# A two-layer hybrid backbone: a lagged start, a later place for layer 1's modulation, and S5 in two streams

## The chip, the cores and the metric

The kernel runs on one core of a Trainium2 chip. PE (TensorE) does the matmuls, DVE (VectorE) and ACT (ScalarE) the elementwise work, POOL (GpSimd) little, and SP (SyncE) issues most DMAs. Times are device microseconds of one execution; the metric is the median over several.

## The reference, cut to what matters

512 tokens (256 of context, 256 latent) of width 1024 pass through two layers, all in fp32. Each layer reads six modulation vectors, computed from a conditioning vector for the latent tokens and another for the context:

```
m = silu(c) @ w_mod[l] + b_mod[l]                    # 6 x 1024, w_mod[l] is 1024 x 6144
p = (rms(x) * norm_mix[l] * (1 + m[1]) + m[0]) @ w_in[l]   # split among three mixers and three gates
y = (s5(p), retention(p), gla(p))                    # scans forward and backward, latent after context
x = x + m[2] * (sum_b sigmoid(gate_b) * (y_b @ w_b)) @ w_out[l]
h = rms(x) * norm_ffn[l] * (1 + m[4]) + m[3]
x = x + m[5] * ((silu(h @ w1) * (h @ w2)) @ w_ffn_out[l])
```

In layer 1 only the latent tokens are needed from the mixers on. A final RMSNorm ends it. "Vector lm" below is modulation vector m of layer l: vector 05 is m[5] of layer 0.

## The kernel before

**Products.** A large fp32 product is made from three reduced-precision ones: operand and weight are split into hi and lo, and hi·hi, hi·lo and lo·hi are accumulated in one bank. A weight tile of 128 x 1024 is loaded into one of three `raw` buffers, ACT writes its hi half, DVE subtracts for its lo half (four pairs), and PE uses both. The activations lie in `rb`, hi and lo.

**What sets the order.** Work is written in program order with priorities, and a scheduler that keeps a modelled time per engine settles each engine's order when the program is built. Loads are issued far ahead (`W_AHEAD`). SP's queue is in order, so a load that waits for its buffer holds back all behind it. `issue_after(x)` keeps the instructions inside it behind instruction x on the same engine.

**The start.** `layer(0)` takes four chunks c of 256 columns. `mod_chunk` loads two 1 MB pieces of `w_mod` (vectors 1 and 0), makes their product with silu(c) on PE, evicts the row by ACT and transposes it. `norm_chunk` transposes the normalised tokens, applies scale and shift on DVE in a buffer `h32`, copies the hi half by ACT and subtracts the lo half. `pack_weights` and `pack_mms` then load and multiply chunk c of the first packed input projection into four banks. `pack_out` evicts them and permutes S5's inputs for a trip through DRAM (`perm`, by DVE from the bank). `load_params2` and `s5_tables` (tables of the S5 scan) follow.

**Modulation vectors on the side.** Vectors 02 to 05 and all of layer 1, besides the S5 tables' rotation and preparation (`rot`, `prep0`, `prep1`), are generators in a list, `side`. `tick`, called in the loops over weights, advances the first of them by one step, `need(name)` drains up to a name. One step of `mod_vec` loads 128 rows of `w_mod` (0.5 MB) into a ring of two tiles `wm`. For vectors 04, 05 and 12 to 15 (`ON_VECTOR`) DVE then accumulates it (one or two operations), and PE sums over partitions at the end (`unit`); for the others PE multiplies it with silu(c) directly. The order was 02, 03, 04, 05, 12, 11, 10, 13, prep1, 14, 15.

**Mixers.** `weave` advances the generators of S5 (`s5_core`, two halves hf of eight groups, one after the other), retention and GLA in turn, one step each. In layer 1 the gates' matmuls lie between them on PE. A half of `s5_core` multiplies inputs by tables, rotates, scans twice, rotates back, and its readout on PE needs both states.

**Layer 1's FFN.** `norm_t` transposes the scaled tokens of one block of 128 (t = 2, 3), applies scale and shift by ACT (half of the columns) and DVE, copies hi by ACT and subtracts lo. `ffn_in_tok` multiplies blocks t in the order (1, 0), i.e. 3 then 2. `ffn_out` runs two passes over the weights in layer 0, one for each half of the tokens, and each ends in `residual` on DVE.

## Time and profile before

| | |
|---|---|
| median of 3 runs | 1385.05 us (1379.94 to 1386.57) |
| profiled execution | 1389.15 us |
| its span | 1387.1 us |
| mean granted clock of PE | 0.986 |
| PE busy | 1332.2 us, 96% |
| DVE busy | 909.6 us, 66% |
| ACT busy | 579.1 us, 42% |
| moved by DMA | 255.63 MB, 184 GB/s |

A timeline row gives the start, the length, the engine, line, operation, result <- operands and count, and in brackets how long the engine was idle before it and what released it. PE's rows overlap, because matmuls are pipelined; the distance of starts tells the pace. PEclk is the granted clock as a share of full speed.

### The profile page before, as it was taken

What the parts mean: (1) busy time and instruction counts of PE and PEld (TensorE: products, weight loads), DVE (VectorE), ACT (ScalarE), POOL (GpSimd) and SP (SyncE); (2) the same over time, 40 slices, a digit from 0 to 9 for tenths busy, and PEclk for the clock granted to TensorE, in tenths of its full rate; (3) what the DMA queues carried; (4) which work ended last, traced back from release to release, by engine and by line L of the source; (5) the groups of instructions that cost most, each with busy time, mean ns of one, the idle gap of its engine ahead of it and who ended that gap; (6) DMA issues with size and microseconds to landing.
All of it is one profiled execution on the core that took longest, in us unless ns stands there. A gap on an engine that the chain in (4) does not pass through costs nothing.

```text
span 1387.1 us, 20296 instructions
## 1 busy us (share of the span) xinstructions
PE 1332.2 (96%) x7723; PEld 1082.7 (78%) x7723; DVE 909.6 (66%) x1395; ACT 579.1 (42%) x920; POOL 73.7 (5%) x115
## 2 busy tenths in 40 slices
PE   4899999999999999999999999999999989899997
PEld 3788888777767778788777777898987867788886
DVE  4579682849879665535455687764696688655555
ACT  3367352333432233222222345544456544544453
POOL 3310000002000020000000000000000010000000
PEclk9999999999999999999999999999999989999999
DMA  9743455677877565633333787654655646465653
GB/s 308 205 123 106 153 167 165 228 220 236 280 245 216 200 184 170 215 92 106 119 115 116 250 310 245 197 158 122 181 160 189 199 145 213 149 194 187 213 183 106
DMA packets 202584, 255.63 MB, mean 184 GB/s; under 512 B 20704, under 2 KB 153100, under 8 KB 201976
## 3 DMA queue, kind: packets, MB, share of 16 engines
q1 hardware_dynamic: 189032, 228.05, 52.6%
q10 hardware_dynamic: 10240, 20.39, 4.1%
q0 software_dynamic: 3216, 5.91, 1.7%
q8 instruction: 61, 1.00, 0.3%
q14 instruction: 35, 0.29, 0.1%
HBM read 231.00 MB, written 23.30 MB: 183 GB/s over the span
## 4 chain that ended last, share of the span: by engine, by line
PE 81%; DMA 8%; DVE 5%; issue 2%; ACT 2%; SPq 1%; POOL 0%; DVEq 0%; ACTq 0%; POOLq 0%
PE b L243 79%; DMA wm<-in_w_mod_dram 4%; PE b L253 2%; DVE arena L231 1%; DVE zone L234 1%; DVE lo L231 1%; DMA arena<-in_w_mod_dram 1%; DMA raw<-in_w_in_dram 1%; ACT arena L228 1%; DMA arena<-udr 1%; ACT hi L228 1%; DMA arena<-sw 1%; DMA arena<-in_ctx_dram 0%; DMA raw<-in_w_ffn_out_dram 0%; DMA rb<-k 0%
## 5 line engine op out<-in xcount | busy, mean ns | idle before, releaser
L243 PE MATMUL b<-hi,rb 128*128 128x512 f32 (+2 forms) x1752 | 535.5, 383 | 5.5 <-DVE arena L593 3.5
L243 PE MATMUL b<-rb,hi 128*128 128x512 f32 (+1 forms) x1568 | 465.3, 378 | 1.4 <-DVE rb L231 1.4
L231 DVE TENSOR_TENSOR lo<-raw,hi 128x1024 fp32r<-128x1024 f32 (+3 forms) x295 | 333.7, 1136 | 201.4 <-ACT hi L228 198.5
L228 ACT ACTIVATE hi<-raw 128x1024 fp32r<-128x1024 f32 (+3 forms) x295 | 289.7, 989 | 419.4 <-PE b L243 275.0
L243 PEld LDWEIGHTS b<-hi,rb 128*128 128x128 f32 x1752 | 328.1, 189 | 67.4 <-issue 8.1
L243 PE MATMUL b<-lo,rb 128*128 128x512 f32 (+2 forms) x876 | 334.2, 382 | 0.9 <-DVE lo L231 0.9
L243 PEld LDWEIGHTS b<-rb,hi 128*128 128x128 f32 x1568 | 284.5, 189 | 64.5 <-issue 11.9
L243 PE MATMUL b<-rb,lo 128*128 128x512 f32 (+1 forms) x784 | 294.2, 376 | 0.0
L243 PEld LDWEIGHTS b<-lo,rb 128*128 128x128 f32 x876 | 166.2, 190 | 28.3 <-issue 1.6
L243 PEld LDWEIGHTS b<-rb,lo 128*128 128x128 f32 x784 | 147.9, 189 | 28.6 <-issue 3.4
L228 ACT ACTIVATE arena<-b 128x512 f32<-128x512 f32 (+7 forms) x168 | 79.1, 481 | 106.1 <-PE b L243 71.8
L243 PE MATMUL b<-arena 128*128 128x96 f32 (+9 forms) x1056 | 120.7, 289 | 0.8 <-ACT arena L228 0.8
L231 DVE TENSOR_TENSOR arena<-arena 128x512 f32<-128x512 f32 (+5 forms) x164 | 102.0, 640 | 17.2 <-ACT arena L228 14.9
L243 PEld LDWEIGHTS b<-arena 128*128 128x128 f32 (+6 forms) x1056 | 89.9, 160 | 24.3 <-issue 8.3
L234 DVE SCALAR_TENSOR_TENSOR arena<-arena,b 128x512 f32<-128x512 f32 (+1 forms) x124 | 72.3, 587 | 47.4 <-PE b L243 44.3
L234 DVE SCALAR_TENSOR_TENSOR zone<-wm,sil,zone 128x1024 f32<-128x1024 f32 x56 | 71.0, 1280 | 26.1 <-DMA wm<-in_w_mod_dram 26.0
L231 DVE TENSOR_TENSOR zone<-zone 128x512 f32<-128x512 f32 (+3 forms) x117 | 67.9, 604 | 28.5 <-DMA wb<-zone 17.4
L228 ACT ACTIVATE rb<-arena 128x256 fp32r<-128x256 f32 (+3 forms) x101 | 46.4, 476 | 61.5 <-PE b L243 33.6
L231 DVE TENSOR_TENSOR rb<-arena,rb 128x256 fp32r<-128x256 f32 (+2 forms) x106 | 53.7, 521 | 16.9 <-ACT rb L228 16.7
L253 PE MATMUL b<-cst,arena 128*128 128x128 f32 (+2 forms) x254 | 40.0, 284 | 19.4 <-DMA arena<-in_norm_mix_dram 8.9
L253 PEld LDWEIGHTS b<-cst,arena 128*128 128x128 f32 (+2 forms) x254 | 30.9, 146 | 27.3 <-issue 16.1
L228 ACT ACTIVATE arena<-arena 128x512 f32<-128x512 f32 (+3 forms) x62 | 36.7, 599 | 34.9 <-DVE arena L231 27.8
(145 smaller groups left out, 686.5 us busy)
## 6 DMA issues: line engine op xcount, KB each, us to landing
wm<-in_w_mod_dram SPq DMA_DIRECT2D x80, 512.0 KB
raw<-in_w_ffn_out_dram SPq DMA_DIRECT2D x66, 512.0 KB
raw<-in_w_in_dram SPq DMA_DIRECT2D x48, 512.0 KB
raw<-in_w_ffn_in_dram SPq DMA_DIRECT2D x44, 512.0 KB
raw<-in_w_ffn_in_dram SPq DMA_DIRECT2D x88, 256.0 KB
raw<-in_w_in_dram SPq DMA_DIRECT2D x48, 384.0 KB
raw<-in_w_out_dram SPq DMA_DIRECT2D x16, 512.0 KB
arena<-in_w_mod_dram SPq DMA_DIRECT2D x7, 1024.0 KB
```

What stands on the lines that cost most here:

```text
L228: self.S.activation(out, in_, f, bias=bias, scale=scale)
L231: self.last = self.V.tensor_tensor(out=out, in0=a, in1=b, op=op).ins
L234: self.last = self.V.scalar_tensor_tensor(out=out, in0=a, scalar=s, in1=b, op0=op0, op1=op1).ins
L243: self.last_mm = self.P.matmul(out, l, r, start=start, stop=stop, **k).ins
L253: self.last_tr = self.P.transpose(out, in_, self.ident[:k, :k]).ins
```

## The change

1. *Start.* The eight loads of `mod_chunk` become sixteen of half the rows. In the loop the packed matmuls lag one chunk: modulation and norm of chunk c, then `pack_mms` of c-1. Chunk c's weights and their splits stay behind the eviction of its modulation row on ACT. `norm_chunk` lets ACT write hi straight from the bank with scale and shift, while DVE makes h32 and lo. `load_params2` and `s5_tables` stand behind the last packed matmul on PE, the tables on ACT behind the last norm.
2. *Modulation.* The order is 02, 03, 04, 05, 11, 10, 12, 13, prep1, 14, 15; those from 12 on are closed until step 2 of layer 0's `ffn_in`, and their instructions stand behind that step's DVE instruction.
3. *Layer 1's packing.* The perm copies read ACT's SBUF copy in place of the bank.
4. *Mixers of layer 1.* Two S5 generators, one for each half, the second three rounds late, and retention first; part of the second half's buffers lie in `zone`.
5. *Layer 1's FFN norm.* hi is written from the bank by ACT; in the first piece of `ffn_in_tok` each block's products with the weights come block by block, the block's lo last.

```diff
@@ act, tick, aside
+        self.closed = ("mod12", "mod13", "prep1", "mod14", "mod15")
+        self.behind = None
...
     def tick(self):
-        if self.side:
-            with self.inside(self.zone):
+        if self.side and not (self.closed and self.side[0][0] in self.closed):
+            with self.inside(self.zone), self.tc.issue_after(self.behind) if self.behind else nullcontext():
@@ mod_chunk
         for m in (1, 0):
             ws[m] = (self.zone if c == 3 and m else self.arena).new(KD, 256)
-            self.q["modc"].dma_start(out=ws[m].ap, in_=i["w_mod"][0][:, D * m + 256 * c:D * m + 256 * c + 256].rearrange(
-                "(k p) c -> p k c", p=128))
+        for kh in range(2):
+            for m in (1, 0):
+                self.q["modc"].dma_start(out=ws[m].ap[:, 4 * kh:4 * kh + 4], in_=i["w_mod"][0][
+                    512 * kh:512 * kh + 512, D * m + 256 * c:D * m + 256 * c + 256].rearrange("(k p) c -> p k c", p=128))
...
         self.act(rows.ap, b[:, :128], AF.Copy)
+        self.row_out = self.last_act
@@ norm_chunk
-            self.tt(hv, b.rearrange("p (t k c) -> p t k c", t=2, k=2), bc(self.mod[:, 0, 1]), ALU.mult)
-            self.tt(hv, hv, bc(self.mod[:, 0, 0]), ALU.add)
-        self.act(self.rb[:, 1:5, 0, ks], h32.ap, AF.Copy)
-        self.tt(self.rb[:, 1:5, 1, ks], h32.ap, self.rb[:, 1:5, 0, ks].bitcast(F32), ALU.subtract)
+            for k in range(2):
+                kk = 2 * c + k
+                src = b[:, 256 * k:256 * k + 256].rearrange("p (t c) -> p t c", t=2)
+                self.act(self.rb[:, rows, 0, kk], src, AF.Identity, scale=sc[:, kk, s:s + 1], bias=sh[:, kk, s:s + 1])
+                self.ts(h32.ap[:, :, k], src, sc[:, kk, s:s + 1], sh[:, kk, s:s + 1], ALU.mult, ALU.add)
+            self.tt(self.rb[:, rows, 1, ks], h32.ap, self.rb[:, rows, 0, ks].bitcast(F32), ALU.subtract)
@@ norm_t
-                if k < 2:
-                    self.act(dst, src, AF.Identity, scale=sc[:, kk, s:s + 1], bias=sh[:, kk, s:s + 1])
-                else:
-                    self.ts(dst, src, sc[:, kk, s:s + 1], sh[:, kk, s:s + 1], ALU.mult, ALU.add)
-            self.act(self.rb[:, 1 + t, 0, ks], h32.ap[:, ks], AF.Copy)
+                self.act(self.rb[:, 1 + t, 0, kk], src, AF.Identity, scale=sc[:, kk, s:s + 1], bias=sh[:, kk, s:s + 1])
+                self.ts(h32.ap[:, kk], src, sc[:, kk, s:s + 1], sh[:, kk, s:s + 1], ALU.mult, ALU.add)
@@ pack_out
-            perm(up.ap[:, c0:], banks[x][:, c0:])
+            perm(up.ap[:, c0:], (o.ap if lean else banks[x])[:, c0:])
@@ ffn_in
+            if f == 2 and l == 0:
+                self.closed, self.behind = (), self.last
             self.tick()
@@ ffn_in_tok, first piece
-                self.tok_mms(banks, ws, (1, 0), range(KD), 0, KD - 1, h)
+                for t in (1, 0):
+                    for k in range(KD):
+                        for x in range(2):
+                            self.mm_(banks[t], h(t, k)[0], ws[k // 2][x][:, k % 2], k == 0 and x == 0, False)
+                    for k in range(KD):
+                        self.mm_(banks[t], h(t, k)[1], ws[k // 2][0][:, k % 2], False, k == KD - 1)
@@ layer
                 for c in range(4):
                     self.mod_chunk(c, brow)
                     self.norm_chunk(c, xs)
-                    self.pack_mms(banks, self.pack_weights(0, 0, c), c)
+                    with self.tc.issue_after(self.row_out):
+                        ws.append(self.pack_weights(0, 0, c))
+                    if c:
+                        self.pack_mms(banks, ws[c - 1], c - 1)
+                self.pack_mms(banks, ws[3], 3)
...
-            self.asides("2345cbadpef")
+            self.asides("2345bacdpef")
...
-        self.weave(("srg", "rsg")[l], g=gla, s=self.s5_core(l, self.s5d[l], u_dr, t0),
-                   r=self.ret(l, rqk, rv, ro, t0))
+        if last:
+            self.weave("rstg", g=gla, s=core(0), t=self.late(3, core(1)), r=ret)
+        else:
+            self.weave("srg", g=gla, s=core(0, 1), r=ret)
```

**ACT at the start, chunks 1 to 3.** `raw` and `hi` are a weight tile and its split half (chunk 0's is the first), `b_249`, `b_343` and `b_437` before are the banks of the modulation rows of chunks 1, 2 and 3. Before:

```order
L228 ACTIVATE hi_313<-raw_310 128x16x48
L228 ACTIVATE hi_313<-raw_310 128x16x16
L228 ACTIVATE arena<-b_249 128x128
L228 ACTIVATE rb<-arena 128x4x256
L228 ACTIVATE hi_407<-raw_404 128x16x48
L228 ACTIVATE hi_407<-raw_404 128x16x16
L228 ACTIVATE hi_501<-raw_498 128x16x48
L228 ACTIVATE hi_501<-raw_498 128x16x16
L228 ACTIVATE arena<-b_343 128x128
```

And now, with the rows of chunks 1, 2 and 3 in `b_231`, `b_331` and `b_431`:

```order
L230 ACTIVATE arena<-b_231 128x128
L230 ACTIVATE hi_301<-raw_298 128x16x48
L230 ACTIVATE hi_301<-raw_298 128x16x16
L230 ACTIVATE rb<-b_278,mod 128x2x128
L230 ACTIVATE rb<-b_288,mod 128x2x128
...
L230 ACTIVATE arena<-b_331 128x128
L230 ACTIVATE hi_401<-raw_398 128x16x48
L230 ACTIVATE hi_401<-raw_398 128x16x16
L230 ACTIVATE rb<-b_378,mod 128x2x128
...
L230 ACTIVATE arena<-b_431 128x128
L230 ACTIVATE hi_501<-raw_498 128x16x48
```

Each row's eviction now stands ahead of its chunk's split; before, chunk 2's stood behind two of them.

**SP at vector 05's last loads.** A merge weight tile is loaded in three pieces (`w_br_...`). Before, the last two steps of vector 05 are `wm_3280` and `wm_3316`, and `wm_3403` is vector 12's first:

```order
L273 DMA raw_3588<-in_w_br_gla_dram 128x3x128
...
L357 DMA wm_3280<-in_w_mod_dram 128x1024
L273 DMA raw_3636<-in_w_br_s_dram 128x2x128
L273 DMA raw_3636<-in_w_br_ret_dram 128x3x128
L273 DMA raw_3636<-in_w_br_gla_dram 128x3x128
L357 DMA wm_3316<-in_w_mod_dram 128x1024
L357 DMA wm_3403<-in_w_mod_dram 128x1024
```

And now, where they are `wm_3304` and `wm_3340`:

```order
L359 DMA wm_3268<-in_w_mod_dram 128x1024
L275 DMA raw_3525<-in_w_br_s_dram 128x2x128
L275 DMA raw_3525<-in_w_br_ret_dram 128x3x128
L275 DMA raw_3525<-in_w_br_gla_dram 128x3x128
...
L359 DMA wm_3304<-in_w_mod_dram 128x1024
L359 DMA wm_3340<-in_w_mod_dram 128x1024
L275 DMA raw_3576<-in_w_br_s_dram 128x2x128
```

Three merge weight tiles fewer stand ahead of vector 05's last load. In PE's order, counted in 512-column matmuls, vector 05's final matmuls stood at 1052, and the tile just ahead of its last load was used from 1134 on; now at 995 and 1062. Vector 11's products stood from 1197 to 1398 and vector 10's from 1446 to 1542; now from 1022 to 1182 and from 1230 to 1398.

**PE at the end of layer 1's mixers.** `rb,hi` and `hi_...` rows with 512 columns are the gates' matmuls, rows that read only `arena` are GLA's, `b_8544<-rb,arena` (now `b_8570`) is S5's readout. Before:

```order
L243 MATMUL b_8417<-arena 128x256 x2
L243 MATMUL b_9141<-hi_9163,rb 128x512 x2
...
L243 MATMUL b_8421<-arena 128x256 x2
L243 MATMUL b_8425<-arena 128x96 x2
L243 MATMUL b_8456<-arena,rb 128x64 x8
L243 MATMUL b_9141<-lo_9200,rb 128x512
...
L243 MATMUL b_8425<-arena 128x96 x6
L243 MATMUL b_8467<-arena,rb 128x64 x8
L243 MATMUL b_8478<-arena 128x128 x2
L243 MATMUL b_9218<-hi_9221,rb 128x512 x2
...
L243 MATMUL b_8516<-arena 128x96
L243 MATMUL b_8544<-rb,arena 32x128 x20
```

And now:

```order
L245 MATMUL b_8486<-arena 128x256 x2
L245 MATMUL b_9244<-hi_9265,rb 128x512
...
L245 MATMUL b_9243<-hi_9265,rb 128x512
L245 MATMUL b_8490<-arena 128x256 x2
L245 MATMUL b_8494<-arena 128x96 x2
L245 MATMUL b_8512<-arena 128x128 x2
L245 MATMUL b_8494<-arena 128x96 x6
L245 MATMUL b_8516<-arena 128x128 x2
L245 MATMUL b_8520<-arena 128x96
...
L245 MATMUL b_8570<-rb,arena 32x128 x7
...
L245 MATMUL b_8570<-rb,arena 32x128 x4
L255 MATMUL b_8600<-cst,arena 128x64 x4
```

Before, gate matmuls stood between the steps of GLA's last chunk (from place 3608 to 3660); now its state stands at 3653 and all later steps in one piece behind place 3660, ahead of S5's readout's end.

## Rows read from the trace of the kernel before

**Rows 1.** The page's first part: busy us, share of the span, instructions.
```profile
PE 1332.2 (96%) x7723; PEld 1082.7 (78%) x7723; DVE 909.6 (66%) x1395; ACT 579.1 (42%) x920; POOL 73.7 (5%) x115
```

**Rows 2.** The windows: stretch, length, busy by engine, PEclk, DMA share, GB/s.
```profile
0.00:35.00 35.00, 15.94 (x214) 12.62 (x215) 15.73 (x45) 11.58 (x26) 13.30 (x29) 1.00 1.00 308
35.00:70.00 35.00, 31.11 (x236) 25.39 (x237) 19.17 (x41) 10.74 (x17) 10.84 (x21) 0.90 0.72 207
...
105.00:140.00 35.00, 33.21 (x215) 30.77 (x214) 32.45 (x59) 25.73 (x41) 2.21 (x4) 1.00 0.38 118
...
385.00:420.00 35.00, 32.00 (x155) 23.93 (x154) 28.27 (x31) 10.85 (x16) 0.00 (x0) 0.95 0.74 234
...
770.00:840.00 70.00, 69.85 (x365) 54.18 (x364) 53.12 (x63) 30.71 (x48) 0.00 (x0) 1.00 0.86 290
...
1120.00:1155.00 35.00, 30.59 (x157) 24.22 (x158) 29.91 (x54) 17.96 (x36) 3.76 (x2) 0.86 0.51 168
```

**Rows 3.** PE's timeline from 8 to 66 us: start, length, work, idle before.
```profile
41.35 1.07 PE L243 MATMUL b<-arena,sil 128*32 128x128 f32 x30
44.90 0.48 PE L253 MATMUL b<-cst,arena 128*128 128x128 f32 x1 [2.47 <-ACT arena L228]
...
47.01 0.65 PE L243 MATMUL b<-wm,one 1*32 1x128 f32 x8
...
51.63 0.33 PE L253 MATMUL b<-cst,arena 128*128 128x128 f32 x1 [0.40 <-ACT arena L228]
...
54.91 0.50 PE L243 MATMUL b<-rb,hi 128*128 128x512 f32 x1 [1.02 <-DVE rb L231]
...
59.55 1.30 PE L243 MATMUL b<-rb,hi 128*128 128x512 f32 x5
...
65.00 0.35 PE L243 MATMUL b<-hi,rb 128*128 128x416 f32 x1
```

**Rows 4.** ACT's timeline from 40 to 53 us.
```profile
43.54 1.15 ACT L228 ACTIVATE hi<-raw 128x768 fp32r<-128x768 f32 x2 [7.21 <-DMA raw<-in_w_in_dram]
44.59 0.26 ACT L228 ACTIVATE arena<-b 128x128 f32<-128x128 f32 x1
```

**Rows 5.** PE's timeline at vector 05 and at vector 10.
```profile
405.33 0.64 PE L243 MATMUL b<-zone,unit 128*32 128x256 f32 x8 [2.23 <-DVE zone L234]
...
517.08 0.64 PE L243 MATMUL b<-wm,sil 128*32 128x256 f32 x8 [1.78 <-DMA wm<-in_w_mod_dram]
```

**Rows 6.** SP's queue at 399 us and DVE's timeline from 399 to 412 us.
```profile
399.24 2.55 SPq L357 DMA_DIRECT2D wm<-in_w_mod_dram  x2
...
403.99 2.48 DVE L234 SCALAR_TENSOR_TENSOR zone<-wm,sil,zone 128x1024 f32<-128x1024 f32 x2 [1.43 <-DMA wm<-in_w_mod_dram]
```

**Rows 7.** PE's timeline between layer 0's two passes of ffn_out.
```profile
845.37 0.50 PE L243 MATMUL b<-hi,rb 128*128 128x512 f32 x1 [1.07 <-DVE arena L231]
```

**Rows 8.** PE's timeline behind the packing of layers 0 and 1.
```profile
109.24 0.44 PE L243 MATMUL b<-hi,rb 128*128 128x384 f32 x1 [1.79 <-DVE arena L593]
...
972.06 0.41 PE L243 MATMUL b<-hi,rb 128*128 128x384 f32 x1 [1.70 <-DVE arena L593]
```

**Rows 9.** PE's timeline at the end of layer 1's mixers.
```profile
1121.86 1.93 PE L243 MATMUL b<-rb,arena 128*32 128x128 f32 x32 [3.00 <-DVE arena L231]
```

**Rows 10.** DVE's timeline in the same place.
```profile
1112.34 2.33 DVE L1122 TENSOR_TENSOR_SCAN arena<-arena 128x512 f32<-128x512 f32 x2
...
1120.36 1.44 DVE L231 TENSOR_TENSOR arena<-arena 64x504 f32<-64x504 f32 x3
```

**Rows 11.** PE's timeline at layer 1's FFN norm.
```profile
1186.54 1.06 PE L253 MATMUL b<-cst,arena 128*128 128x128 f32 x8 [1.79 <-DVE arena L238]
1190.01 1.94 PE L253 MATMUL b<-cst,arena 128*128 128x128 f32 x8 [2.41 <-DVE arena L238]
1191.61 0.78 PE L243 MATMUL b<-hi,rb 128*128 128x512 f32 x1
```

**Rows 12.** DVE's groups by line and shape: count, busy us, mean ns, idle before.
```profile
L231 DVE TENSOR_TENSOR arena<-arena 128x512 f32<-128x512 f32 x118 | 79.3, 685 | 15.2 <-ACT arena L228 14.5
```

More of the change, by code (lines that the diff above doesn't have):

```diff
@@ L227, in act @@
     def act(self, out, in_, f, scale=1.0, bias=0.0):
-        self.S.activation(out, in_, f, bias=bias, scale=scale)
+        self.last_act = self.S.activation(out, in_, f, bias=bias, scale=scale).ins
     def tt(self, out, a, b, op):
@@ L406, in weave, with late @@
                         del gens[c]
+    @staticmethod
+    def late(n, gen):
+        for _ in range(n):
+            yield
+        yield from gen
     def aside(self, name, gen):
@@ L598, in pack_out @@
             self.act(o.ap[:, c0:], banks[x][:, c0:], AF.Copy)
-            perm(up.ap[:, c0:], banks[x][:, c0:])
+            if lean and x == 0:
+                self.act(o.ap[0:64, 0:256], banks[0][0:64, 0:256], AF.Copy)
+            perm(up.ap[:, c0:], (o.ap if lean else banks[x])[:, c0:])
             for s in range(2):
@@ L1077, in s5_core @@
         nn = 64 - n0
-        u8 = self.new(16, 64)
-        for hf in range(2):
+        for hf in hfs:
+            u8 = self.new(8, 64)
             gs = slice(8 * hf, 8 * hf + 8)
@@ L1112, in s5_core @@
             c, s = rot.ap[:, 0], rot.ap[:, 1]
-            rr, ri, t = big.new(8, 64), big.new(8, 64), big.new(8, 64)
+            tmp = self.zone if l and hf else big
+            rr, ri, t = tmp.new(8, 64), tmp.new(8, 64), tmp.new(8, 64)
             self.tt(rr.ap, X[0].ap, c, ALU.mult)
@@ L1128, in s5_core @@
                 self.tt(ri.ap, X[1].ap, b_, ALU.mult)
-                o = self.new(8, 64)
+                o = big.new(8, 64) if x else tmp.new(8, 64)
                 nc.vector.memset(o.ap[0:64, :, 0:1], 0.0)
@@ L1148, in s5_core @@
             self.read_out = self.last_mm
-            if hf == 0:
-                yt = self.yt = self.new(8, 128)
+            if hf == hfs[0] and hfs[0] == 0:
+                self.yt = self.new(8, 128)
+            yt = self.yt
             for gg in range(ng):
```

39 lines of the change are left out of this document (22 added, 17 removed).

## The prediction

> **What bounds the kernel now.** I read the busy times on the page first [rows 1]: PE is busy 1332.2 of 1387.1 us, no other engine above 909.6. The change neither removes nor adds a large matmul, so all it can win are the gaps of PE and the stretches in which PE's granted clock is halved. The table of windows [rows 2] then shows where those are: 35 to 70 us (PE 31.11 of 35, clock 0.90), 105 to 140, 385 to 420 (32.00), and 1120 to 1155 (30.59, clock 0.86). The timeline gives each gap its releaser. From start to start, the 24 512-column matmuls between 59.55 and 65.00 us take 227 ns each [rows 3]. I call that one unit, and count places in PE's order in it.
>
> The profiled execution took 1389.15 us (span 1387.1), 4.10 above the median of 1385.05. The sum is made against 1389.15, and 4.1 is taken off at the end.
>
> **The start (0 to 65 us).** Before, chunk 2's row eviction on ACT stood behind the hi split of chunk 3's weights. That split waited 7.21 us for its DMA, until 43.54, and the eviction followed at 44.59 [rows 4], so PE began chunk 2's transposes at 44.90 after 2.47 idle [rows 3]. Now ACT evicts chunk c's row ahead of that chunk's hi split, and PE has the packed matmuls of chunk c-1 behind chunk c's modulation. What can be won between 41.35 and 65.00 us (23.65 us)? The rows from 44.90 to 51.63 stand in the stretch of halved clock: the norm took 2.11 and modulation 3 took 4.62 [rows 3], half of which is 1.05 and 2.3. At full clock the work between 41.35 and 65.00 is then 1.0 of modulation 2, two norms of 1.05, 2.3 and two chunks of 5.45: 16.3. The rest, 7.3 us, is idle time (2.47, 0.40, 1.02) and half clock. Modulation 3's weights stand ahead of the load that ended 43.54, so they were there by then, and in the new order PE still has chunk 1's or 2's matmuls to do while they land. I take **-7.3**. The ends are -3 (only the two waits of 2.47 and 1.02 go, less a new one of 0.5 on ACT) and -9 (a finish at about 56, modulation 3 at 41.8 with 2.3, 5.45, 1.05 and 5.45 of work from there, 14.3). The norm of a chunk drops the copy of 1024 columns on ACT and two passes on DVE, and evicts straight from the bank. Four evictions of 256 take the copy's place. PE covers both. The DVE work of the S5 tables starts when packing ends. It shifts along as long as it is not itself the bound: DVE is busy 32.45 of 35 us in 105 to 140 [rows 2], which is the first rival.
>
> The w_mod chunks now come in halves, eight more DMAs. In the first 35 us the DMA share is 1.00 at 308 GB/s [rows 2], with transfers of 1 MB and less mixed in one queue, so the row shows no gap that more transfers would add to: zero. The Trainium skill, page "DMA: Bandwidth & Descriptors", section "Anatomy of one DMA", speaks against it: it states a fixed cost near 2.0 us for each DMA beside the bytes, measured on the GpSimd path. Eight of those in series would be 16 us and turn the sum to about 1389; a share of 1.00 says that they overlap.
>
> **The order of the modulations.** Before, vector 12 was built on DVE and vectors 11 and 10 on PE behind it; now 11 and 10 come first, and 12, 13, the S5 preparation, 14 and 15 wait for the third step of layer 0's FFN. Each step has its price:
> - Vector 10's last loads no longer run into the FFN. PE's wait of 1.78 for one of them at 517.08 [rows 5] goes: **-1.9** with its restart.
> - Vector 05's final matmuls move from unit 1052 to 995, 57 earlier. The load that was waited for (issued 399.24, used by DVE from 403.99 after a wait of 1.43, PE idle 2.23 before 405.33 [rows 5, 6]) moves too. It stood behind a merge weight used at unit 1134, 82 units after its own use, and now stands behind one used at 1062, 67 after: 15 units or 3.4 us more time. The waits there are 2.8 in all. I take **-1.5**, between -2.8 and +3 (DVE does not keep up, 28.27 of 35 busy [rows 2]).
> - Vector 11 on PE reads its loads directly, in the stretch where DMA is 0.74 busy. The ring holds two tiles, so a load is issued when the one two places ahead has been used. At four places of the new order that leaves 24 to 26 units, 5.4 to 5.9 us, between that use and the load's own use. Issue to use was 4.75 us in one case [rows 6]. It was more where PE waited at 517.08 [rows 5]. So **+1.5**, from 0 to +4.
> - The closed work lands in the FFN. DVE instructions of 1.24 us each [rows 6] (8 for vector 12) leave the crowded merge and go where nothing waits for them. In ffn_out the loads of 14 and 15 now cross the boundary of the two passes, where DMA is 0.86 busy at 290 GB/s and PE already waited 1.07 before 845.37 [rows 2, 7]. Zero; it costs up to +5 if the cover is gone (second rival).
>
> **Layer 1's packing.** The copies that held a bank until DVE had them now read SBUF, and ACT frees the bank. PE's 1.70 before 972.06 [rows 8] falls to about 0.5: **-1.2**, from -1.7 to 0. Layer 0 keeps its own wait of 1.79 before 109.24, since nothing there changes.
>
> **S5 in two streams.** Before, the second half's DVE steps came last (scans 1112.34, its differences 1120.36 [rows 10]), and PE waited 3.00 for them at 1121.86 [rows 9]. Now that half runs beside the first, three rounds later, so the 3.00 goes. But GLA's last state matmuls move from unit 3608 to 3653, and the gate matmuls that filled PE end at unit 3660. Where 52 units lay between the steps of GLA's last chunk, 7 are left. PE then waits for GLA itself. The nearest row is the wait of 3.00 that S5 had in this place; the far end is a whole S5 half on DVE (10 operations at 0.685 [rows 12], 2.33 of scans, twice 1.44 [rows 10]: 12.1). I take 4 against the 3.00, **+1**, from -3 to +9.
>
> **Layer 1's FFN norm.** The hi half is written from the bank by ACT without an intermediate, and the first products with lo come last. PE waited 1.79 and 2.41 for scaled rows ahead of 1186.54 and 1190.01, and its first FFN matmul came at 1191.61 [rows 11]. The first block's matmuls can now start before the second block's transposes, but in the order only two of them do; the second block's transposes still wait for DVE's scaling. **-2.5**, from 0 to -4.2.
>
> **Sum.** -7.3 -1.9 -1.5 +1.5 -1.2 +1 -2.5 = -11.9. 1389.15 - 11.9 = 1377.25, and less 4.1 it is **1373**.
>
> **Rivals.**
> *The start's gain is lost again behind it.* DVE is 93% busy from 105 to 140 us [rows 2], and PE's wait of 1.79 at 109.24 [rows 8] is DVE's. If the tables are not released earlier by the full 7.3, only the slack of 2.55 of that window stays, and vector 05's matmuls, 13 us earlier, wait 3 longer instead of 1.5 less. That is +4.75 and +4.5: **1382**. For it: the rows of DVE. Against it: DVE was only 19.17 of 35 busy in 35 to 70, so what queues there starts as soon as its input does.
>
> *The boundary in ffn_out.* The loads of vector 15 and its steps of 1.24 on DVE meet the residuals, which DVE also makes; four steps more ahead of them are +5, **1378**. For it: DMA 0.86, DVE 53.12 of 70 [rows 2]. Against: the number of loads in the stage stays.
>
> *The change does not do what it says at the start:* the lagged matmuls wait for their own splits, which now stand behind the rows on ACT; -3 in place of -7.3, and the norm wins nothing: +6.8, **1380**. Against: even chunk 3's split began at 43.54 [rows 4], and its matmuls come last.
>
> *Eight halves cost eight whole transfers.* At 308 GB/s a half takes 1.7 us [rows 2]; eight more of those ahead of chunk 3 put 13.6 on the start: **1387**. A share of 1.00 speaks against it.
>
> *GLA's last chunk stands bare.* With both S5 streams ahead of it in each round on DVE, GLA ends later by a whole half, 12.1, on top of the 4, and the clock falls once more: 0.90 over the window 35 to 70 is a loss of 3.5 us [rows 2]. 12.1 + 4 + 3.5 against 3.00 is +16.6 in place of +1: **1389**, within 0.5%. For it: the new order of PE. Against it: DVE has 29.91 of 35 in that window now, and what it does in total stays.
>
> *Slower: PE waits for vectors 11 and 10 load by load.* With a ring of two, each load is issued only when PE has used the one two places ahead; in the stretch of 0.74 DMA share each of the eight loads of vector 11 then holds PE up by what one did at 517.08, 1.78 [rows 5], 14.2 in all, and the clock falls twice for it, 3.5 each [rows 2]: +21.2 in place of +1.5 is **1393**. It decides against the change from about 13 us of such waits. For it: DVE's wait of 1.43 for one of these loads, which PE now has itself [rows 6]. Against it: only four of the sixteen have under 6 us.
>
> **How the numbers follow.** Chances: forecast 0.57, start lost behind 0.15, boundary 0.08, not what it says 0.07, halves 0.02, GLA bare 0.05, load by load 0.06. The forecast's own range runs from 1361 (start -9, vector 05 -2.8, S5 -3, norm -4.2) to 1380 (start -3, vector 11 +4). To leave no more than 2 in 10 out it goes up to 1385, which takes in the first three rivals with their spread. 0.5% (6.9 us) is what a measurement of this kernel can tell from no change, so faster means under 1378.1 and slower over 1392. Faster: 0.57 without its upper end of 0.05, half of the boundary and the lower spread of the first and third (0.09): 0.65. Slower: load by load and the upper end of GLA bare, 0.08. Same 0.27.
>
> **What would show it.** Right at the start: ACT evicts rows 2 and 3 within a microsecond of PE's modulation, the first matmul of gla_v comes near 57.7 in place of 65.00, and the window 35 to 70 has PE above 33. Wrong: an idle row of several us at the perms near 100, or the window 105 to 140 with more PE idle than 1.8. Modulations: no row of PE waiting for wm near 508, none above 1 us at vector 05, and those of vector 11 below 2 in all. S5: the wait ahead of S5's readout gone, and PE's waits from GLA's last state matmuls to its output add up to 3 to 6. FFN norm: the first FFN matmul 4 to 5 us after the last matmul of the projection. The forecast is wrong altogether if the start moves by less than 3 us.

## The result, and the profile after

The changed kernel takes **1403.82 us** (median of 12 runs, 1393.38 to 1409.58) against 1386.24 of the kernel before in the same comparison: ratio 1.0128, 95% interval 1.0100 to 1.0155. It is slower by 1.3%, where 1373 (1361 to 1385) was forecast. Its profiled execution took 1393.38 (span 1391.3) and was the shortest of the twelve; a second profile, of another execution, took 1403.31 (span 1401.1), which is near the median. The profile of before has a span of 1387.1. Single executions differ: beside the second profile the kernel before took 1396.24 once.

The first part of the page, the first profile, then the second (as [rows 1]):

```profile
PE 1338.3 (96%) x7723; PEld 1083.0 (78%) x7723; DVE 913.1 (66%) x1407; ACT 585.1 (42%) x940; POOL 78.8 (6%) x115
```
```profile
PE 1348.1 (96%) x7723; PEld 1091.7 (78%) x7723; DVE 913.0 (65%) x1407; ACT 585.5 (42%) x940; POOL 78.9 (6%) x115
```

Subtract from the spans: PE was idle 54.9 us before, and 53.0 and 53.0 in the two profiles. **The change did win idle time, 1.9 us. PE's busy time grew instead**, by 6.1 and by 15.9 us, for the same 7723 matmul records. The trace's clock records tell how much of this is clock. Of its busy time PE spent 27.3 us at half clock before, 28.0 in the first profile and 55.6 in the second. If half of such time is lost (an estimate), the clock makes about 14 of the 15.9 us in the second profile, the typical one, and next to nothing of the 6.1 in the first. What those 6.1 are stays open; they are spread over many groups of matmuls. The windows of the first profile (as [rows 2]):

```profile
35.00:70.00 35.00, 31.57 (x222) 26.30 (x215) 24.06 (x61) 13.28 (x24) 8.58 (x17) 0.95 0.69 211
...
385.00:420.00 35.00, 33.01 (x184) 22.23 (x183) 19.47 (x25) 10.68 (x17) 0.00 (x0) 1.00 0.70 212
...
770.00:840.00 70.00, 68.47 (x353) 52.51 (x352) 52.31 (x66) 31.30 (x51) 0.00 (x0) 1.00 0.79 276
...
1120.00:1155.00 35.00, 31.37 (x186) 24.18 (x186) 26.71 (x49) 18.11 (x35) 3.42 (x2) 0.90 0.34 111
```

I compared the traces by place (the count of 512-column units in PE's order, taken at the first large matmul there): how much later than before PE comes through each stretch, in us. A stretch need not hold the same work in both kernels, since small matmuls change places.

| places | what lies there | forecast | first profile | second profile |
|---|---|---|---|---|
| 0–100 | start | −7.3 | −2.9 | −2.6 |
| 100–800 | layer 0's packing and mixers | 0 | +2.1 | +0.9 |
| 800–2900 | vectors: merge, FFN, boundary | −1.9 | −5.0 | −2.4 |
| 2900–3300 | layer 1's packing | −1.2 | +0.1 | 0.0 |
| 3300–3600 | layer 1's mixers | +1 with the next row | +11.8 | **+13.6** |
| 3600–3700 | their end, with GLA's last chunk | | −4.1 | **+3.2** |
| 3700–end | FFN norm, FFN | −2.5 | +2.0 | +1.2 |
| sum | | −11.9 | +4.1 | +14.0 |

The mixers' +7.7 and +16.8 are larger than all the other terms together. Part of the +11.8 and of the −4.1 is work that has changed places: 28 records of small matmuls more stand ahead of place 3600 and 28 fewer behind it. Two things are new. Ahead of place 3600 PE waits 4.3 us in both profiles instead of 0.8, and the clock is halved for 10.2 and 13.7 us where it had been full. Behind place 3600 it is halved for 6.8 and 23.9 us, before for 10.2. So the first profile has its loss ahead of place 3600 alone, and the second on both sides. The window 1000 to 1030 of before, then of the second profile (columns as in [rows 2]):

```profile
1000.00:1030.00 30.00, 29.22 (x195) 25.42 (x194) 26.05 (x48) 15.54 (x24) 0.91 (x1) 1.00 0.55 159
```
```profile
1000.00:1030.00 30.00, 27.48 (x135) 24.06 (x135) 19.19 (x35) 14.21 (x21) 0.00 (x0) 0.77 0.64 176
```

PE's timeline behind place 3600, the first profile, then the second; both rows hold the same 70 records of small matmuls of GLA's last chunk (the built order has 42 matmuls of it, the trace 84 records):

```profile
1111.47 9.03 PE L245 MATMUL b<-arena 48*128 48x256 f32 x70 [0.93 <-DVE arena L236]
```
```profile
1115.41 14.57 PE L245 MATMUL b<-arena 48*128 48x256 f32 x70 [1.58 <-DVE arena L236]
```

### The profile page after: what moved, and what is told of

Read it like the earlier page. It is cut to its first block, busy times and chain, and to the rows that moved or that the text cites. A ratio compares the mean times of both kernels' runs of the same rounds, so it can differ in the third digit from the quotient of the medians.

```text
span 1391.3 us, 20310 instructions
## 1 busy us (share of the span) xinstructions
PE 1338.3 (96%) x7723; PEld 1083.0 (78%) x7723; DVE 913.1 (66%) x1407; ACT 585.1 (42%) x940; POOL 78.8 (6%) x115
## 4 chain that ended last, share of the span: by engine, by line
PE 56%; DVE 5%; DMA 5%; ACT 3%; issue 2%; SPq 0%; POOL 0%; DVEq 0%; POOLq 0%; ACTq 0%
PE b L245 55%; DVE lo L233 2%; DMA raw<-in_w_ffn_out_dram 1%; PE b L255 1%; ACT arena L230 1%; ACT hi L230 1%; DVE arena L233 1%; DMA wm<-in_w_mod_dram 1%; DMA raw<-in_w_in_dram 1%; DVE arena L242 1%; DVE arena L236 1%; DMA raw<-in_w_out_dram 0%; DVE rb L233 0%; DMA udr<-arena 0%; DMA raw<-in_w_br_s_dram 0%
## 5 line engine op out<-in xcount | busy, mean ns | idle before, releaser
L245 PE MATMUL b<-arena 128*128 128x96 f32 (+8 forms) x1064 | 121.7, 289 | 1.3 <-DVE arena L236 0.9
L230 ACT ACTIVATE arena<-b 128x256 f32<-128x256 f32 (+7 forms) x170 | 79.4, 480 | 102.5 <-PE b L245 75.5
L245 PEld LDWEIGHTS b<-arena 128*128 128x128 f32 (+5 forms) x1064 | 91.5, 161 | 25.1 <-issue 8.3
L233 DVE TENSOR_TENSOR arena<-arena 128x512 f32<-128x512 f32 (+4 forms) x162 | 102.3, 645 | 10.4 <-ACT arena L230 8.4
L233 DVE TENSOR_TENSOR zone<-zone 128x512 f32<-128x512 f32 (+4 forms) x122 | 70.5, 605 | 22.7 <-DMA wb<-zone 15.2
L233 DVE TENSOR_TENSOR rb<-arena,rb 128x256 fp32r<-128x256 f32 (+1 forms) x110 | 54.3, 506 | 22.1 <-ACT rb L230 22.0
L230 ACT ACTIVATE rb<-arena 128x256 fp32r<-128x256 f32 (+3 forms) x93 | 40.0, 442 | 52.5 <-PE b L245 38.9
L505 POOL TENSOR_TENSOR st<-st,mh 128x1 f32<-128x1 f32 x16 | 16.4, 1025 | 646.4 <-DVE st L242 645.3
```

Source lines behind the costliest of these rows:

```text
L230: self.last_act = self.S.activation(out, in_, f, bias=bias, scale=scale).ins
L233: self.last = self.V.tensor_tensor(out=out, in0=a, in1=b, op=op).ins
L245: self.last_mm = self.P.matmul(out, l, r, start=start, stop=stop, **k).ins
L505: self.G.tensor_tensor(out=st[:, 3:4], in0=st[:, 2:3], in1=self.mh[:, 0:1], op=ALU.pow)
```

## The experiments

The parts are numbered as in the change: P1 start, P2 vectors, P3 layer 1's packing, P4 two S5 streams, P5 FFN norm. "GLA" is the place of GLA's last state matmuls in the built order of PE, and in brackets how many small matmuls of that chunk stand behind place 3655, when the gates' matmuls (which end at 3660) are all but used up. "Halved" is how long the trace's records have the granted clock at 1.2 instead of 2.4 GHz, in the profiled execution, at places 3300 to 3600 and at places 3600 to 3700.

| kernel | parts | GLA | halved to 3600, us | halved from 3600, us | ratio to before, 95% |
|---|---|---|---|---|---|
| before | – | 3608 (28) | 0 | 10.2 | 1 |
| after, first and second profile | 1 2 3 4 5 | 3653 (42) | 10.2, 13.7 | 6.8, 23.9 | 1.0128 (1.0100–1.0155) |
| u1_start_as_before | 2 3 4 5 | 3653 (42) | 13.7 | 27.3 | 1.0143 (1.0087–1.0200) |
| u2_vectors_as_before | 1 3 4 5 | 3653 (42) | 10.2 | 23.9 | 1.0165 (1.0126–1.0203) |
| u3_change_without_packing | 1 2 4 5 | 3660 (60) | 13.7 | 27.3 | 1.0096 (1.0068–1.0124) |
| u4_one_s5_stream | 1 2 3 5 | 3631 (46) | 10.2 | 20.5 | 1.0115 (1.0068–1.0162) |
| u5_ffn_norm_as_before | 1 2 3 4 | 3653 (42) | 10.2 | 23.9 | 1.0110 (1.0063–1.0158) |
| k125_without_both | 1 2 5 | 3608 (28) | 0 | 10.2 | 1.0050 (1.0026–1.0073) |
| a1_only_start, two profiles | 1 | 3608 (28) | 0, 0 | 6.8, 10.2 | 1.0072 (1.0044–1.0100) |
| a2_only_vectors | 2 | 3608 (28) | 0 | 6.8 | 1.0018 (0.9998–1.0038) |
| a3_only_packing | 3 | 3631 (46) | 10.2 | 17.1 | 1.0057 (1.0037–1.0077) |
| a4_only_two_s5_streams | 4 | 3660 (60) | 3.4 | 27.3 | 1.0116 (1.0088–1.0144) |
| a5_only_ffn_norm | 5 | 3608 (28) | 0 | 10.2 | 1.0033 (1.0012–1.0053) |
| srg_before_weave | none, weave order only | 3660 (76) | 0 | 27.3 | 1.0074 (1.0049–1.0098) |
| s4_fill_in_readout_wait | none, fillers only | 3608 (28) | 0 | 3.4 | 1.0004 (0.9979–1.0029) |

The theory to start with was that the forecast's rival "GLA's last chunk stands bare" had come true; against it stood the start, the vectors and the norm.

### One part undone

Each kernel is the changed one with the lines of one part as they were:

```diff
@@ u1: layer, mod_chunk and norm_chunk as before, e.g.
-                    if c:
-                        self.pack_mms(banks, ws[c - 1], c - 1)
+                    self.pack_mms(banks, self.pack_weights(0, 0, c), c)
@@ u2: order and closing as before
-            self.asides("2345bacdpef")
+            self.asides("2345cbadpef")
@@ u4: one S5 generator in layer 1
-            self.weave("rstg", g=gla, s=core(0), t=self.late(3, core(1)), r=ret)
+        self.weave(("srg", "rsg")[l], g=gla, s=self.s5_core(l, self.s5d[l], u_dr, t0), r=self.ret(l, rqk, rv, ro, t0))
@@ u5: norm_t and the first piece of ffn_in_tok as before
-                        self.mm_(banks[t], h(t, k)[1], ws[k // 2][0][:, k % 2], False, k == KD - 1)
+                self.tok_mms(banks, ws, (1, 0), range(KD), 0, KD - 1, h)
@@ u3: perm from the bank as before
-            perm(up.ap[:, c0:], (o.ap if lean else banks[x])[:, c0:])
+            perm(up.ap[:, c0:], banks[x][:, c0:])
```

> The change with the start as before (whole w_mod loads, no lag, norm through the buffer). The profile after shows the start 2.9 us ahead at place 100. Theory A: this run is 3 us slower than the change, ratio 1.013 to 1.017. Rival C, that the start's new order disturbs what follows it up to layer 1 (the scheduler moves other work): it is 3 us or more faster, ratio 1.010 or below.

> The change with the modulation vectors in the old order and never closed. Theory A: the moved vectors won 5 to 9 us up to the FFN's end of the first pass and gave about 5 back behind it, so without them the time is 0 to 6 us longer than the change, ratio 1.013 to 1.017. Rival B, that these loads and the DVE steps behind them make the loss: 8 us or more shorter, ratio 1.007 or below.

> The change with layer 1's S5 in one stream again (the weave as before, both halves in one generator). Theory A, that the two streams cost the time in layer 1: in the profile after, PE is 6.1 us ahead of before at place 3300 of its order and 4.1 behind at place 3600, so this run should be 8 to 15 us faster than the change, 1389 to 1396 us where the change has 1404, ratio to before 1.002 to 1.007. Rival B, that the moved modulation vectors cost it: no more than 3 us faster, ratio 1.010 or above.

> The change with layer 1's FFN norm and the first piece of its FFN as before. In the profile after the norm lost 1.2 us where 2.5 less were forecast. Theory A: the norm is worth no more than 2 us either way, ratio 1.011 to 1.015. Rival D, that the new order of the first FFN piece is what costs: 4 us or more faster, ratio 1.010 or below.

None of the first four brought the time back: all lie 1.1% to 1.7% above before. Undoing the two streams did not even undo the move of GLA. Its place is 3631, not 3608, because the lean packing moves it too. That had not been thought of, so the packing was taken out next, and then both.

> The change without the packing part alone. GLA's last chunk stands wholly behind the gates' end because of the two S5 streams. Theory L in its general form: still slower than the kernel without both by 6 to 14 us, ratio 1.000 to 1.008. Rival, that the packing is the only cause: 0.991 to 0.997.

> The change without the packing part and without the two S5 streams: the start, the order of the modulation vectors and the FFN norm. Its order on PE at the mixers' end is that of before. Theory L: 5 to 12 us faster than before, ratio 0.991 to 0.997, since the start brought 2.9 us and the vectors some 6 in the profile after. Rival C, that these parts cost the clock as well: 1.000 or above.

Without the packing alone GLA stands fully bare (60) and the loss stays. Without packing and streams GLA is back at 3608, the halved time at these places is that of before, and 1.0128 falls to 1.0050. So packing and streams together make 0.78 of the 1.28%. The gain of 5 to 12 us that was expected of what remains did not come: about half a percent of loss is left.

### One part alone

Each is the kernel before with one part's lines from the diff ahead of the prediction.

> The kernel before with one part of the change alone: layer 1's perm copies read ACT's SBUF copy. All four runs so far kept this part and all were 1.1 to 1.65% slower than before. Its order on PE has GLA's last state matmuls at place 3631 instead of 3608 and most of the last chunk behind the gates' end at 3660. Theory L, that this part moves GLA's chain out of its cover and that the granted clock halves there: ratio to before 1.004 to 1.011, with 10 us of halved clock near 1000 us and 20 near 1112 us. Rival S, that the two S5 streams are the cause: 0.998 to 1.001.

> The kernel before with layer 1's S5 in two streams alone. In its order on PE all of GLA's last chunk stands behind the gates' end at place 3660. Theory L in its general form (GLA's chain without cover costs the clock, whichever part moves it): ratio 1.004 to 1.012, with a halved clock of 20 us or more near 1112. Rival: DVE's earlier S5 steps make up for it, ratio 0.997 to 1.002.

> The kernel before with the change's start alone. The kernel without packing and two streams was 0.5% slower than before in the median, although its profile was 4.9 us shorter. Theory P: the start keeps the 2.8 us of the profiles at place 100 and loses 0 to 3 of them again: ratio 0.997 to 1.001. Rival C: the start is what brings the 0.5%, 1.003 or above.

> The kernel before with the modulation vectors' new order and closing alone. Theory P: 8.5 us less up to the end of the FFN's input projection (no product of a vector on PE there any more), 4 more at the boundary of ffn_out: ratio 0.995 to 0.999. Rival C: the vectors bring the 0.5% of the kernel without packing and two streams, 1.003 or above.

> The kernel before with layer 1's FFN norm and first FFN piece of the change alone. In all profiles with this part PE waits some 4 us once for the second block's scaling instead of 1.8 and 2.4 twice. Theory P: 0 to 2 us slower, ratio 0.999 to 1.002. Forecast's value: 2.5 us faster, 0.998. Rival C: 1.003 or above.

No part is faster alone, and the start, the vectors and the norm lie above the ranges expected of them. The packing, three lines, did remove the wait of [rows 8], and loses 0.57%, with GLA moved by 23 places. The two streams lose 1.16%; the same row of 70 records, shape by shape, runs wholly at the lower clock and takes 1.8 times the 9.03 us above (PE's timeline):

```profile
1108.99 16.19 PE L243 MATMUL b<-arena 48*128 48x256 f32 x70 [2.60 <-DVE arena L234]
```

The five ratios add up to about 3.0% over 1, more than the whole change loses. P3 and P4 cost 1.73% one by one and 0.78% together, which fits that both pay for the same place; P1, P2 and P5 cost 1.23% one by one and 0.50% together, which nothing here explains.

### The order alone

This is the kernel before, with layer 1's weave taking S5 ahead of retention. No instruction is added or removed.

```diff
-        self.weave(("srg", "rsg")[l], g=gla, s=self.s5_core(l, self.s5d[l], u_dr, t0),
+        self.weave(("srg", "srg")[l], g=gla, s=self.s5_core(l, self.s5d[l], u_dr, t0),
```

> The kernel before with one string changed: layer 1 weaves its mixers in the order S5, retention, GLA instead of retention, S5, GLA. No instruction is added or removed; in the order on PE, GLA's last state matmuls move from place 3608 to 3660, where the gates end. Theory L (what costs is GLA's last chunk without gate matmuls around it, whichever edit puts it there, and the granted clock that halves in it): ratio to before 1.007 to 1.014, with 20 us or more of halved clock near 1112 us. Rival: it is the packing's or the two streams' own instructions, so here 0.998 to 1.002.

It is slower by 0.74%. The window 1100 to 1145 of before, then of this kernel (columns as in [rows 2], PEclk third from the end):

```profile
1100.00:1145.00 45.00, 40.30 (x262) 32.01 (x262) 35.88 (x67) 21.77 (x43) 3.76 (x2) 0.89 0.41 137
```
```profile
1100.00:1145.00 45.00, 41.83 (x265) 33.45 (x266) 33.63 (x69) 18.07 (x40) 3.76 (x2) 0.70 0.35 117
```

PE is *busier*, and its clock is 0.70 instead of 0.89. The groups by shape between 1100 and 1130 have the same form of matmul at both prices (count, busy us, mean ns; before, then this kernel):

```profile
L243 PE MATMUL b<-arena 128*128 128x96 f32 x28 | 4.6, 285 | 0.0
```
```profile
L243 PE MATMUL b<-arena 128*128 128x96 f32 x32 | 9.3, 448 | 0.0
```

So the order alone, without an instruction of the change, can cost the clock; the weave's order moves all three mixers, and it is GLA's small matmuls that run at half clock. In PE's timeline 74 records of them stand in one row of 17.31 us; before, the longest such row there was one of 32:

```profile
1106.17 17.31 PE L243 MATMUL b<-arena 48*128 48x256 f32 x74
```

### Work put into the wait

This is the kernel before with 13 superfluous 512-column matmuls ahead of layer 1's second S5 readout, whose bank the readout then overwrites.

```diff
             b = self.bank()
             ng = 128 // nn
+            if l and hf:
+                for _ in range(13):
+                    self.mm_(b, self.rb[:, 4, 0, 0], self.rb[:, 4, 0, 0:4], True, True)
```

> The kernel before with 13 extra 512-column matmuls on PE (13 x 0.227 = 2.95 us) ahead of layer 1's second S5 readout, where PE waited 3.00 us for the scan; their sums are overwritten by the readout. Theory clock by demand: the granted clock falls there for the 10.2 us because PE did little just before; with the wait filled it falls later, shorter or not at all: 0.997 to 0.9985 (2 to 4 us less), the halved stretch at 1119.6 gone or under 7 us. Rival, the clock does not depend on what fills the wait: ratio 1.000 to 1.001, the stretch stays 10 us.

PE's timeline there, to set beside [rows 9], where 32 readout matmuls took 1.93 us behind a wait of 3.00:

```profile
1111.18 3.23 PE L243 MATMUL b<-rb 128*128 128x512 f32 x13
...
1116.17 1.35 PE L243 MATMUL b<-rb,arena 128*32 128x128 f32 x40
```

The wait is gone, 40 readout records take 1.35 us, and the halved stretch is 3.4 us instead of 10.2. In the nine profiles with GLA at place 3608 and no fillers (before, k125, a2, a5, two of a1, and three of the start's edits below) it is 6.8 or 10.2 us. So what PE does in this place has a part in the clock, as the theory said, though this rests on one profile. The gain is small: places 3600 to 3700 take 52.1 us, the fillers included, where before took 53.1. The time is the same (1.0004, up to 1.0029): eight of the twelve runs took 1380.1 to 1386.1 and four 1391.6 to 1393.8. The forecast of 2 to 4 us less is not borne out by the median.

### The three edits of the start, one at a time

```diff
@@ s1_halves_only: the sixteen half loads of mod_chunk
+        for kh in range(2):
@@ s2_norm_only: hi from the bank in norm_chunk
+                self.act(self.rb[:, rows, 0, kk], src, AF.Identity, scale=sc[:, kk, s:s + 1], bias=sh[:, kk, s:s + 1])
@@ s3_lag_only: pack_mms one chunk late, loads and tables behind
+                    if c:
+                        self.pack_mms(banks, ws[c - 1], c - 1)
```

> The kernel before with one edit: each 1 MB modulation load of the four chunks at the start is issued as two halves. If the start's late loss (a1_only_start, 1.0072) comes from the number and order of the loads: ratio 1.004 to 1.007 here. If halves are the gain and the rest of the start is the loss: 0.996 to 0.999, with PE three to five us ahead at place 100.

> The kernel before with one edit: norm_chunk writes the rounded hi half straight from the transposes on ScalarE and makes the residual on VectorE from a second pass. If this is the loss of the start: 1.003 to 1.007, since ScalarE has eight more instructions a chunk that stand between the weight splits. If it is a gain as the prediction had it: 0.997 to 1.000.

> The kernel before with one edit: the packing matmuls of chunk c run one chunk late, the weights' loads behind the modulation row, and the parameter loads and S5 tables behind the last packing matmul. If the lag is the loss: 1.003 to 1.007, by S5's tables and the vectors' turns coming later between places 300 and 1000. If not: 0.997 to 1.001.

All three lose: 1.0252 (1.0224–1.0280), 1.0081 (1.0061–1.0101) and 1.0078 (1.0050–1.0106). At place 100 they stand 6.3 us behind, 1.5 behind and 4.1 ahead of before; seven other kernels with the start of before are 1.3 to 2.0 ahead there too. So the lag does win 2 to 3 us at the start, and the halves without it do harm. PE's waits for the modulation loads (total, times, longest; to 200 us, before and with halves) did fall:

```profile
PE b L243 <- DMA arena<-in_w_mod_dram: 8.4, 2, 6.2
```
```profile
PE b L243 <- DMA arena<-in_w_mod_dram: 1.5, 2, 1.0
```

But ACT now meets a table of S5 ahead of chunk 3's row, and PE waits 2.3 us for ACT there, besides 3.9, 3.0 and 3.0 us for DVE elsewhere up to 200 us, where it had been 1.8 and 1.0 (ACT's timeline with halves, where 8.27 us are spent on a load of `s_log_dt`, and the row's eviction follows at 59.02):

```profile
58.05 0.23 ACT L228 ACTIVATE zone<-zone 128x32 f32<-128x32 f32 x1 [8.27 <-DMA zone<-in_s_log_dt_dram]
...
59.02 0.26 ACT L228 ACTIVATE arena<-b 128x128 f32<-128x128 f32 x1
```

What the start loses behind it is likely the same mechanism once more, in layer 0. The scheduler, with other modelled times at the start, puts layer 0's small mixer matmuls in other places. Matmuls outside the large products, by place in the built order:

| kernels | 520–600 | 600–640 | 640–700 | 700–720 |
|---|---|---|---|---|
| before, a2, a3, a5, srg | 60 | 68 | 78 | 54 |
| a1, k125, u4 | 116 | 54 | 146 | 12 |
| after, u2, u3, u5 | 116 | 54 | 144 | 30 |
| s1 | 116 | 42 | 138 | 16 |
| s2, s3 | 100 | 62 | 142 | 20 |
| a4, u1 | 60 | 68 | 58 | 116 |

Every edit of the start crowds them, and so do the two streams of layer 1 in a4 and u1. From place 600 to 700 PE needs 54 us before and 70 to 76 in the kernels with a changed start; most of that is only work that has changed places. Between 200 and 330 us the clock is never halved in the six profiles with the order of before here (s4 is the sixth); with another order it is in eight of fourteen, for 3.4 to 34.1 us. But the first profile of the start alone, of k125 and of others shows none, so this is not shown to be the whole loss.

### The changed kernel and its start, profiled again

Both are the kernels as they were, in another execution.

> The changed kernel itself. Its profiled execution was the shortest of twelve (1393.4 against a median of 1403.8). Theory clock: a typical execution has the same waits, and its 10 us more are halved clock in the two stretches where small matmuls of the mixers stand together, places 520 to 700 of PE (layer 0) and 3600 to 3700 (layer 1): 1400 to 1408 us, 30 to 50 us halved there, the sum of PE's waits within 2 us. Rival, waits differ: the clock as before and some wait longer by 5 us or more.

> The start alone once more (median 1393.35, its profiled execution the shortest at 1382.69). Theory clock: 1390 to 1400 us with 20 us or more halved at places 540 to 800, where 72 of the small matmuls of layer 0's mixers now stand at 520 to 580 (before 44), and PE's waits unchanged. Rival, waits differ: as above.

The second profile of the changed kernel has 9.8 us more span, 9.8 us more busy PE, and 53.0 us idle as the first. PE's busy time at half clock is 27.6 us more, which is enough to explain it; 7.3 us of it lie at places 3600 to 3700. Layer 0's mixers have no part in it: between 200 and 330 us the second profile shows no halved clock, against what was expected. The start alone took 1392.88, 10.2 us longer, with the clock halved for 10.2 us at 287.7 (places 600 to 700) where the first profile had none: 3.8 us there. PE's idle time grew too, from 51.1 to 54.7, so the rival had a part in this one. The window 285 to 330 of its first profile, its second, then of u1 (the longest of its four executions) and a4, which have the same order there:

```profile
285.00:330.00 45.00, 44.05 (x277) 31.69 (x277) 37.38 (x62) 17.33 (x26) 10.68 (x6) 1.00 0.74 233
```
```profile
285.00:330.00 45.00, 43.88 (x248) 30.27 (x248) 32.86 (x53) 15.59 (x24) 8.04 (x4) 0.89 0.64 205
```
```profile
285.00:330.00 45.00, 45.00 (x225) 32.04 (x225) 19.89 (x34) 7.89 (x13) 0.00 (x0) 0.62 0.44 133
```
```profile
285.00:330.00 45.00, 44.87 (x321) 33.11 (x320) 31.35 (x53) 13.57 (x21) 4.63 (x3) 1.00 0.77 243
```

One and the same order can pass at 1.00 or at 0.62; so the crowding at most sets how much is at stake, not what each execution does. What decides that stays open.

## Why the prediction was wrong, point by point

**S5 in two streams: the term that failed (+1; measured +7.7 and +16.8, with the packing).** The prediction saw GLA's last state matmuls move from place 3608 to 3653 and priced it as a wait, 4 against 3.00, with nothing for the clock. Behind place 3600 the waits came out a little below that: 3.00 went, 0.93 and 1.58 came at the row of 70, and the wait behind the readouts is 2.08 and 1.62 where it had been 1.66. What was not priced is the clock, 13.7 us more of it halved there in the second profile, and what happened ahead of place 3600: 3.5 us more of waits and 10.2 and 13.7 us of halved clock. The rival on GLA had the place and the mechanism behind 3600, but it let the time come from a later end of GLA on DVE (12.1) and gave the clock one stretch of 3.5. Between the two profiles 17.1 us more of halved clock cost 7.3 us in this place, so the 24 to 27 us seen in most kernels cost about 10 to 12 (an estimate from these two numbers). Its chance of 0.05 was too low: [rows 9] showed readouts at half pace behind a wait in this very place, in a window of clock 0.86 [rows 2].

**Layer 1's packing (−1.2).** Right in its place: the wait of 1.70 is gone, and both profiles gain 2.0 us across place 3252, where it stood, as the packing alone does. A new wait of 1.36 us in the first profile and 3.4 us of halved clock in the second, both ahead of that place, took most of it back. It was wrong in its sum: GLA's order is the scheduler's answer to the whole stage, and three changed lines moved it. In the changed kernel a wait also came up at GLA's first step. PE's, DVE's and ACT's timelines (first profile): ACT waits for a weight load that stands ahead of the gate's copy, DVE waits for ACT, and PE for DVE:

```profile
1004.21 2.56 PE L245 MATMUL b<-arena,zone 128*128 128x64 f32 x16 [2.78 <-DVE arena L233]
```
```profile
1002.40 0.96 DVE L233 TENSOR_TENSOR lo<-raw,hi 128x768 fp32r<-128x768 f32 x1 [4.98 <-ACT hi L230]
```
```profile
1001.53 0.84 ACT L230 ACTIVATE hi<-raw 128x768 fp32r<-128x768 f32 x1 [6.02 <-DMA raw<-in_w_in_dram]
1002.28 0.47 ACT L230 ACTIVATE gs<-b 128x384 f32<-128x384 f32 x1
```

Behind that the clock is halved for 10.2 and 13.7 us, where it had been 1.00. The packing alone has the same 10.2 there, and so has the change without the two streams (u4); without the packing but with the streams it is 13.7 (u3), and with the streams alone 3.4.

**The start (−7.3; −2.9 and −2.6 at place 100).** That is under the 3 us at which the prediction called itself wrong altogether. About 3.4 of the 7.3 was half clock, the stretch from 44.4 us in the one execution it was read from. None of the seven other kernels with the start of before has the clock halved there, and they reach place 100 1.3 to 2.0 us earlier than that profile. So the change itself is worth about 1 us. The rival "not what it says" gave −3. The waits of 2.47 and 0.40 went, but that of 1.02 became 3.37, and gla_v came at 62.03, not 57.7:

```profile
55.61 0.50 PE L245 MATMUL b<-rb,hi 128*128 128x512 f32 x1 [3.37 <-DVE rb L233]
...
62.03 0.43 PE L245 MATMUL b<-hi,rb 128*128 128x416 f32 x1
```

DVE and ACT show what was missed: the splits of gla_v's weights (832 columns) now stand among the steps of chunk 3's norm on both.

```profile
52.42 1.02 DVE L233 TENSOR_TENSOR lo<-raw,hi 128x832 fp32r<-128x832 f32 x1 [0.86 <-ACT hi L230]
53.36 0.99 DVE L242 TENSOR_SCALAR arena<-b,mod 128x256 f32<-128x256 f32 x2
54.27 1.28 DVE L233 TENSOR_TENSOR rb<-arena,rb 128x512 fp32r<-128x512 f32 x2
```
```profile
51.49 0.90 ACT L230 ACTIVATE hi<-raw 128x832 fp32r<-128x832 f32 x1 [0.50 <-DMA raw<-in_w_in_dram]
52.29 1.00 ACT L230 ACTIVATE rb<-b,mod 128x256 fp32r<-128x256 f32 x2
```

The rival that the gain is lost behind the start came true in part, though not by DVE between 105 and 140 us as it said: +2.1 and +0.9 by place 800. PE is 10 us later through places 500 to 600 alone, but 244 instead of 124 records of small matmuls stand there now, and most of this comes back by place 800.

**The halves at no cost.** Within the lag this held: no wait for a modulation load of chunks 1 to 3 is over a microsecond. By the Trainium skill, page "DMA: Bandwidth & Descriptors", section "Anatomy of one DMA", a transfer issued on the GpSimd path has a fixed cost near 2.0 us. These loads are issued by SP. With the halves alone PE's waits for them fell from 8.4 to 1.5 us with eight transfers more, so here no such cost adds up in series. The loss of the halves alone is not a wait for them; the waits named above came up beside it.

**The vectors (−1.9; −5.0 and −2.4).** Right in sign in these profiles, but not borne out by the part alone: 1.0018 (0.9998–1.0038) leaves out the 0.9986 of −1.9 us. The wait of 1.78 at vector 10 is gone and the window 385 to 420 runs at 1.00. Vector 05 won little: its wait is 1.89 in the first profile in place of 2.23, and gone in the second. Places 1200 to 2400 are shorter by 7.8 us, of which some 6 is PE work of the vectors and the S5 preparation that now stands in other places (about 23 us of such rows before, 17 after). Places 2400 to 2900, with the boundary of ffn_out, gave 3.4 and 6.5 back. In k125 it shows bare, on PE and on DVE:

```profile
835.58 0.47 PE L245 MATMUL b<-hi,rb 128*128 128x512 f32 x1 [2.93 <-DVE arena L233]
```
```profile
829.74 1.28 DVE L236 SCALAR_TENSOR_TENSOR zone<-wm,sil,zone 128x1024 f32<-128x1024 f32 x1 [2.28 <-DMA wm<-in_w_mod_dram]
```

That is the second rival (+5). The slower rival, waits load by load for vectors 11 and 10, did not happen.

**The FFN norm (−2.5; +2.0 and +1.2).** The first FFN matmul came 5.9 us after the projection's last one instead of 7.3, where 4 to 5 were forecast: one wait of 3.90 took the place of 1.79 and 2.41, behind the same DVE scaling.

```profile
1191.27 1.94 PE L255 MATMUL b<-cst,arena 128*128 128x128 f32 x8 [3.90 <-DVE st L242]
1192.90 0.79 PE L245 MATMUL b<-hi,rb 128*128 128x512 f32 x1
```

Alone, the part is 0.33% slower than before; its profile has this stretch only 0.2 us longer, so where that comes from is not shown.

**The range.** Its lower end of 1361 does not follow from the terms named for it: start −9, vector 05 −2.8, S5 −3 and norm −4.2 take 8.7 us off 1373, which is 1364.

**What stays open.** k125 and a1 keep half a percent and more that their first profiles do not show; these are 5.0 and 6.3 us shorter than the profile of before. The second profile of a1 makes clock in a crowded place a likely cause, with waits beside it. The 6.1 us by which PE's busy time grew in the first profile of the change have no cause shown. Why one execution passes such a place at full clock and another does not was not found. No version that beats the kernel before came out of these runs.

## What to carry to other kernels

Where PE is busy 96% and a change only moves work, compare PE's busy time for the same instruction count before its waits, and then how much of it lies at half clock: here that explains about 14 of 15.9 us in one execution and almost none of 6.1 in another. Where an edit moves small matmuls out from between large ones, or lets a scheduler do so, price their whole row at half the clock (1.8 times as long here), not only the wait ahead of it. Do not credit a change with half clock read from a single execution. And look at the built order of stages that the diff does not touch: a new start re-sorted the mixers more than a hundred microseconds later.

## What the runs showed of the hardware

The granted clock fell to 1.2 GHz while the profile shows PE busy without a gap: in u1 between 285 and 330 us PE is busy 45.00 of 45 at a mean clock of 0.62, with small mixer matmuls in its rows. Identical programs took 1393.38 and 1403.31 us with the same 53.0 us of idle time on PE. A row of 70 small matmul records took 9.03 us at full clock and 16.19 at half, 1.8 times as long and not twice. With thirteen matmuls whose result nobody reads, one halved stretch was 3.4 us, in one profile, where nine without them have 6.8 or 10.2.
